# Moving every SBUF tile of a tuned encoder block to a multiple of 128 bytes

## Chip, cores and metric

The kernel runs on one core of a Trainium2 chip. The metric is the device time of one execution in microseconds (us), as the median of several runs.

## What is computed

One block of a streaming encoder on 1024 tokens of 1024 channels, with 16 meta tokens in front, in float32. Cut to what matters:

```python
def hybrid_mixer(u, w_in, ...):
    a, q, k, v, r, lr, ga, gb = jnp.split(einsum('bld,dn->bln', u, w_in), IN_SPLITS, axis=-1)
    p = multiscale_pool(a)                       # trailing means over 2, 4, 8, 16 positions, minus the token
    y_a = (p @ w_pool_mix, per group, * pool_scale) @ w_pool_out
    log_a = log_sigmoid(lr @ w_gate_up + b_gate) / GLA_TAU
    o = gla_chunked(q * GLA_DK ** -0.5, k, v, log_a)      # 4 heads, chunks of 64
    y_b = (rmsnorm(o, gla_norm) * silu(r)) @ w_gla_out
    return (sigmoid(ga) * y_a + sigmoid(gb) * y_b) @ w_out

def reference(x, meta_tokens, ...):
    h = concatenate([meta, x])
    h = h + hybrid_mixer(rmsnorm(h, norm_mix), ...)
    h = h + square(relu(rmsnorm(h, norm_ffn) @ w_ff1)) @ w_ff2        # 1024 -> 4096 -> 1024
    return rmsnorm(h, norm_final)[:, N_META:]
```

## The kernel before

Every large product is made of float32r matmuls. A float32 operand is split into a rounded part and the rest (`hi`, `lo`; ScalarE copies, VectorE or GpSimd subtracts), and `mm3` (L248) issues three matmuls for one product: L252 hi times hi, L253 hi times lo, L254 lo times hi. The first operand is the weights that are loaded into the array, 128x128; the second moves through it, mostly 128x512. Each matmul loads its weights anew. An output tile is one PSUM bank, 128x512 (`b_sc`, `b_mm`, `b_y`, `b_z`, `b_o`). In the profile a row reads output<-inputs, with the moving operand first or the two sorted together, and a tile that is both is named once.

The stages follow one another in the list `one`, and TensorE's order is written out by hand (`tc.manual_schedule` for PE):

1. `start`, `gate_stage` (to about 220 us): the norm, transposes of x into `th`, `tl`, and the blocks ga, q, r and two of gb, as a Strassen-like scheme of seven products for each pair of blocks (`Quarters`): moving operands are `th0`/`tl0` behind their 16 meta columns, `th1`/`tl1`, and the combinations `P4` to `P7`; weights are the splits in `w1h`, `w1l`.
2. The pooling branch (to about 310 us): `a_block` with 264- and 512-wide pieces of `th`, `mix_block`, `ya_block` with `pm` as the moving operand.
3. `gla` (to about 500 us): the chunked attention, with the blocks k, v, gb and `yb_block` (moving operand `yg`) poured between its steps.
4. `out_tile` (to about 640 us): `wo0`, then `wo1` move, `th`, `tl` are the weights.
5. `ff_layers` (to about 935 us): the first layer of the MLP in `Quarters` again; moving are `th0`, `th1`, `wo0` (reused) and `t4h`, `t4l`; weights `w1h`, `w1l`.
6. `ff2` (to the end): seven products of the second layer; both operands are splits in a ring of seven slots, four in `w1h`, `w1l` and three in `fxh`, `fxl`, so that either may be moving or weights.

SBUF is laid out by two stacks (`Stack`, L35): `left` grows up from the start, `right` down from the end; a tile's address is what was pushed before it. The sizes in a partition that matter here:

```python
ident = left.push("ident", [P, P], F32)          # 512 bytes in a partition
mask = left.push("mask", [P, 6, CH], U8)         # 384
gB = left.push("gB", [P, D], F32)                # 4096
small = left.push("small", [P, 152], F32)        # 608
wgu = left.push("wgu", [16, 256], F32)           # 1024
metab = left.push("metab", [P, 4, 16], F32)      # 256
lrT_meta = left.push("lrT_meta", [16, 16], F32)  # 64
```

Behind them on the left come `raw0`, `raw1`, `w1h`, `w1l`, `th0`, `tl0`, `th1`, `tl1`, and then each stage's tiles; in the first two stages `lrtok` (576 bytes) lies ahead of the others. In the built program `ident` begins at byte 16512, `w1h` at 31648, `th0` at 48032, `P5h` at 123872; the right stack ends at byte 229344, with `fxh` at 219104 and `t4h` at 202720.

Of the kernel before, what the change touches and what calls it, by code (L numbers as in the profile page):

```python
# [7 lines left out]
F32 = mybir.dt.float32  # L8
# [6 lines left out]
P = 128  # L15
# [88 lines left out]
def kernel(  # L104
# [10 lines left out]
    act, dve, pool, pe = nc.scalar, nc.vector, nc.gpsimd, nc.tensor  # L115
    left, right = Stack(tc, "left"), Stack(tc, "right")

    psp, ps_open = {}, []

    def banks(keep=0, **tags):  # L120
# [35 lines left out]
    ident = left.push("ident", [P, P], F32)  # L156
    mask = left.push("mask", [P, 6, CH], U8)
    gB = left.push("gB", [P, D], F32)
    small = left.push("small", [P, 152], F32)
    small_at = [0]  # L160

    def tiny(n):
        a = small_at[0]
        small_at[0] += n
        assert small_at[0] <= 152
        return small[:, a : a + n]

    pscale, bgate, gnorm = tiny(4), tiny(2), tiny(4)
    stat = [tiny(16) for _ in range(4)]
    eps_t = tiny(1)  # L170
    pool.memset(eps_t, EPS)
    wgu = left.push("wgu", [16, 256], F32)
    metab = left.push("metab", [P, 4, 16], F32)
    lrT_meta = left.push("lrT_meta", [16, 16], F32)
    raw = Raw(nc, [left.push(f"raw{i}", [P, D], F32) for i in range(2)])
    W1 = Ring(nc, raw, left.push("w1h", [P, 2, D], F32R), left.push("w1l", [P, 2, D], F32R), 2)
    left_ff = left.mark()
# [14 lines left out]
    def bcast(v):  # L192
        return v[None, :].broadcast_to([P, D])
# [27 lines left out]
    def layer_norm(xt, u):  # L221

        rows = xt.shape[0]
        ss = ln_stat[ln_n[0] % 4][:rows]
        ln_n[0] += 1
        act.activation(u, xt, ACT.Square, accum_out=ss)
        rs = inv_sqrt(ss, 1, 1.0 / D)
        dve.scalar_tensor_tensor(u, xt, rs, gB[:rows], ALU.mult, ALU.mult)
# [3 lines left out]
    def transposed(u, half, at, tags=("ms",), to=None):  # L232
        rows = u.shape[0]
        th, tl = (t[half] for t in to or (TH, TL))
        if rows == P:
            for j in range(2):
                turn_n[0] += 1
                b = bank(tags[turn_n[0] % len(tags)]).rearrange("p (a b) -> p a b", a=4)
                for i in range(4):
                    pe.transpose(b[:, i], u[:, (4 * j + i) * P : (4 * j + i + 1) * P], ident)  # L240
                split_from_psum(th[:, 4 * j : 4 * j + 4, at : at + P], tl[:, 4 * j : 4 * j + 4, at : at + P], b)
        else:
            b = bank("ms")[:, : 8 * rows].rearrange("p (a b) -> p a b", a=8)
            for i in range(8):
                pe.transpose(b[:, i], u[:, i * P : (i + 1) * P], ident[:rows, :rows])
            split_from_psum(th[:, :, at : at + rows], tl[:, :, at : at + rows], b)
# [38 lines left out]
    class Quarters:  # L285
# [9 lines left out]
        def load(self, i, u):  # L295
            dst = self.places[i % 2][u]
            self.w[i, u] = dst.rearrange("p (k c) -> p k c", k=KT)
            nc.sync.dma_start(self.w[i, u], self.block(2 * i + u))
# [103 lines left out]
    S, rings = {}, [W1]  # L402
# [9 lines left out]
    def drive(steps):  # L412

        for ring, aps, fn in steps:
            if fn not in (start, gate_stage):
                for r in rings:
                    r.top_up()
            wbs = [ring.views.pop(ring.done + i) for i in range(len(aps))] if ring else []
            held = len(aps)
            for cost in fn(*wbs) or ():  # L420
                if cost == "free":
                    ring.done, held = ring.done + held, 0
                    for r in rings:
                        r.top_up()
                else:
                    yield cost
            if ring:
                ring.done += held
# [16 lines left out]
    def load_vw(i):  # L445
        vw, n = S["vw"][i], 256 + 16 * (i == 0)
        for j in range(2):
            r = raw.load(w_cols(C_V + i * 256 + j * P), D).rearrange("p (k c) -> p k c", k=KT)
            c = slice(j * P, (j + 1) * P)
            act.activation(vw[:, 0, :, c], r, ACT.Copy)  # L450
            eng = pool if i else dve
            eng.tensor_tensor(vw[:, 1, :, c], r, f32(vw[:, 0, :, c]), ALU.subtract)
        if i == 0:
            r = S["lrraw"]
            act.activation(vw[:, 0, :, 256:], r, ACT.Copy)
            pool.tensor_tensor(vw[:, 1, :, 256:], r, f32(vw[:, 0, :, 256:]), ALU.subtract)
# [3 lines left out]
    def v_tile(i, t):  # L460

        vw, w = S["vw"][i], 256 + 16 * (i == 0)
        if t == 8:
            half, at, n = 0, 0, META
        else:
            half, n = t // 4, P
            at = OFF[half] + (t % 4) * P
        b = bank("mm")[:n, :w]
        mm3(
            b, KT, lambda k: (TH[half][:, k, at : at + n], TL[half][:, k, at : at + n]),  # L470
            lambda k: (vw[:, 0, k], vw[:, 1, k]),
        )
        if i == 0:
            dve.tensor_copy(S["lrtok"][:n, t], b[:, 256:])
        if t == 8:
            act.activation(vm[:, i * 256 : i * 256 + 256], b[:, :256], ACT.Copy)
        else:
            act.activation(S["v"][i][:, t], b[:, :256], ACT.Copy)
# [27 lines left out]
    def turned(u, t):  # L506

        half, at = t // 4, OFF[t // 4] + (t % 4) * P
        for j in range(2):
            b = quad(bank("ms"))  # L510
            for i in range(4):
                pe.transpose(b[:, i], u[:, (4 * j + i) * P : (4 * j + i + 1) * P], ident)
            k = slice(4 * j, 4 * j + 4)
            split_from_psum(TH[half][:, k, at : at + P], TL[half][:, k, at : at + P], b)
            act.activation(S["ut"][half, j][:, :, (t % 4) * P : (t % 4 + 1) * P], b, ACT.Copy)

    def start():
        act.preload_act_table_set("natural_log_exp_and_others")
        S["lrtok"] = left.push("lrtok", [P, 9, 16], F32)
        S["lrraw"] = left.push("lrraw", [P, KT, 16], F32)  # L520
        S["left_x"] = left.mark()
        xs = left.push("xs", [P, 4, D], F32)
        us = left.push("us", [P, 3, D], F32)
        xm = left.push("xm", [META, D], F32)
        um = left.push("um", [META, D], F32)
        mf = left.push("mf", [P, 6, CH], F32)
        S["u2p"] = right.push("u2p", [P, 2, HALF], F32)
        S["fs"] = right.push("fs", [P, 2, HALF], F32)
        q = gate_quarters
        for i in range(2):  # L530
            q.places[i][0] = right.push(f"rawx{i}", [P, D], F32)
        S["right_ut"] = [right.mark()]
        S["ut"] = {}
        for half, j in ((0, 1), (1, 0), (1, 1), (0, 0)):
            S["ut"][half, j] = right.push(f"ut{half}{j}", [P, 4, HALF], F32)
            S["right_ut"].append(right.mark())
        S["vw"] = [right.push("vw0", [P, 2, KT, VP], F32R)]
        load = lambda t: nc.sync.dma_start(xs[:, t % 4], x[t * P : (t + 1) * P, :])
        load(0)
        nc.sync.dma_start(ident, ident_in)  # L540
        nc.sync.dma_start(gB, bcast(norm_mix))
        for t in (1, 2, 3):
            load(t)
        q.load(0, 0)
        m = lambda half, j: tuple(a[half][:, 4 * j : 4 * j + 4, OFF[half] : OFF[half] + HALF] for a in (TH, TL))
        q.x.update({"P1": m(0, 0), "P2": m(0, 1), "P3": m(1, 1)})
        run = S["gate_run"] = q.run()
        for t in range(8):
            if t < 4:
                layer_norm(xs[:, t % 4], us[:, t % 3])  # L550
                turned(us[:, t % 3], t)
                load(t + 4)
                if t == 0:
                    nc.sync.dma_start(S["lrraw"], w_in[:, C_LR : C_LR + 16].rearrange("(k p) c -> p k c", p=P))
                    load_vw(0)
                    q.load(1, 0)
                continue
            if t == 4:
                nc.sync.dma_start(xm, meta)
                q.load(0, 1)  # L560
                q.load(1, 1)
                nc.sync.dma_start(mf, masks)
                q.prime()
                next(run)
                next(run)
                v_tile(0, 0)
            layer_norm(xs[:, t % 4], us[:, t % 3])
            turned(us[:, t % 3], t)
            if t < 7:
                v_tile(0, t - 3)  # L570
            else:
                layer_norm(xm, um)
        next(run)
        transposed(um, 0, 0)
        next(run)
        v_tile(0, 8)
        pool.tensor_copy(mask, mf)
# [78 lines left out]

    one = []
    step(one, start)
    step(one, gate_stage)

# [841 lines left out]
```

## Time and profile before

| | |
|---|---|
| median of 3 runs | 1262.49 us (1261.29 to 1262.67) |
| profiled execution | 1260.3 us, of which the span from first to last instruction 1258.5 us |
| granted TensorE clock, mean | 0.997 |
| TensorE matmuls | 6799, busy 97% of the span |
| VectorE, ScalarE, GpSimd busy | 68%, 50%, 5% |
| DMA | 175.40 MB, 139 GB/s over the span |

The profile is that of one execution. A matmul's busy time is from its start to its modelled end, and matmuls overlap, so the rate of TensorE is read from the distance between starts. A row of groups gives the line, engine, operation, output<-inputs, shapes and count, then the busy time in us and the mean of one in ns, then the idle time ahead of it and what ended that.

### The profile page before, as it was taken

To read this page: it belongs to the slowest core of one execution; us is meant where nothing else is said; L and a number is where in the kernel's file an instruction comes from. 1 tells how busy PE (TensorE), PEld (TensorE's weight loads), DVE (VectorE), ACT (ScalarE), POOL (GpSimd) and SP (SyncE) were. 2 spreads that over 40 slices of the span, in tenths; PEclk is the share of its full clock that TensorE was granted. 3 is DMA by queue.
4 is the path that set the end of the run, shared out by engine and by line. 5 is a ranking of instruction groups with operands and counts; after the bars stand their busy time and mean duration, and the time that the engine had idled before them with its cause. 6 is when DMAs were issued, how large, how long until landed. Compare 5 with 4: busy or idle time off the path is not lost.

```text
span 1258.5 us, 18159 instructions
## 1 busy us (share of the span) xinstructions
PE 1216.6 (97%) x6799; PEld 1001.1 (80%) x6799; DVE 852.4 (68%) x1404; ACT 625.3 (50%) x1101; POOL 58.6 (5%) x37
## 2 busy tenths in 40 slices
PE   3999999999999999999999999999999999999997
PEld 2888888988887787788878888888878788888776
DVE  6776667564365767743897676677764887887686
ACT  7567757431445564422664554554553444445444
POOL 0000000001000115400000000000000000000000
PEclk9999999999999999999999999999999999999999
DMA  8023334427211236851244444543569863323432
GB/s 264 1 67 109 109 95 136 130 70 241 75 35 35 85 116 203 310 175 51 76 143 149 161 151 142 163 155 130 175 228 373 277 213 102 100 93 92 167 92 84
DMA packets 143863, 175.40 MB, mean 139 GB/s; under 512 B 11008, under 2 KB 83472, under 8 KB 143776
## 3 DMA queue, kind: packets, MB, share of 16 engines
q1 hardware_dynamic: 143776, 174.25, 42.7%
q8 instruction: 53, 0.87, 0.3%
q14 instruction: 34, 0.28, 0.1%
HBM read 120.74 MB, written 53.48 MB: 138 GB/s over the span
## 4 chain that ended last, share of the span: by engine, by line
PE 90%; DVE 4%; ACT 2%; DMA 2%; issue 2%; SPq 0%; DVEq 0%; ACTq 0%
PE b_mm L252 9%; PE b_mm L254 9%; PE b_mm L253 9%; PE b_o L253 8%; PE b_o L254 8%; PE b_o L252 8%; PE b_y L252 5%; PE b_y L254 5%; PE b_y L253 5%; PE b_z L252 3%; PE b_z L253 3%; PE b_z L254 3%; PE b_sc L252 3%; PE b_sc L253 3%; PE b_sc L254 3%
## 5 line engine op out<-in xcount | busy, mean ns | idle before, releaser
L252 PE MATMUL b_mm<-th,w1h 128*128 128x512 f32 (+1 forms) x240 | 86.0, 358 | 0.0
L253 PE MATMUL b_mm<-tl,w1h 128*128 128x512 f32 (+1 forms) x240 | 83.8, 349 | 0.0
L254 PE MATMUL b_mm<-th,w1l 128*128 128x512 f32 (+1 forms) x240 | 83.7, 349 | 0.0
L270 ACT ACTIVATE w1h<-raw 128x512 fp32r<-128x512 f32 x96 | 59.6, 623 | 44.0 <-PE b_sc L253 14.2
L252 PE MATMUL b_sc<-th,w1h 128*128 128x512 f32 x192 | 76.7, 399 | 1.9 <-ACT u2p L362 1.9
L252 PE MATMUL b_o<-w1h 128*128 128x512 f32 x192 | 75.3, 392 | 2.7 <-DVE h L1310 1.7
L253 PE MATMUL b_o<-w1l,w1h 128*128 128x512 f32 x192 | 75.0, 390 | 1.3 <-DVE w1l L271 1.3
L253 PE MATMUL b_sc<-tl,w1h 128*128 128x512 f32 x192 | 75.8, 395 | 0.3 <-DVE tl L197 0.3
L254 PE MATMUL b_sc<-th,w1l 128*128 128x512 f32 x192 | 75.7, 394 | 0.0
L254 PE MATMUL b_o<-w1h,w1l 128*128 128x512 f32 x192 | 75.1, 391 | 0.1
L271 DVE TENSOR_TENSOR w1l<-raw,w1h 128x512 fp32r<-128x512 f32 x96 | 65.7, 686 | 11.1 <-ACT w1h L270 11.1
L270 ACT ACTIVATE w1h<-fs 128x512 fp32r<-128x512 f32 x72 | 45.4, 630 | 49.9 <-PE b_y L253 34.3
L252 PE MATMUL b_z<-th,w1h 128*128 128x512 f32 x160 | 62.5, 390 | 0.4 <-DVE c L616 0.4
L253 PE MATMUL b_z<-tl,w1h 128*128 128x512 f32 x160 | 62.4, 390 | 0.4 <-DVE tl L1222 0.4
L254 PE MATMUL b_z<-th,w1l 128*128 128x512 f32 x160 | 62.3, 389 | 0.0
L271 DVE TENSOR_TENSOR w1l<-fs,w1h 128x512 fp32r<-128x512 f32 x72 | 49.4, 686 | 16.2 <-ACT w1h L270 16.1
L1373 DVE TENSOR_TENSOR bt<-w,w 128x512 f32<-128x512 f32 x80 | 54.8, 686 | 2.2 <-DMA w<-in_w_ff_dram 2.2
L270 ACT ACTIVATE w1h<-bt 128x512 fp32r<-128x512 f32 x44 | 27.6, 629 | 55.3 <-issue 31.9
L252 PEld LDWEIGHTS b_mm<-th,w1h 128*128 128x128 f32 x240 | 45.0, 188 | 8.8 <-issue 2.3
L252 PE MATMUL b_mm<-wo,th 128*128 128x512 f32 x128 | 50.7, 396 | 0.0
L254 PE MATMUL b_o<-fxh,fxl 128*128 128x512 f32 x128 | 50.2, 392 | 0.0
L252 PE MATMUL b_o<-fxh 128*128 128x512 f32 x128 | 50.1, 392 | 0.0
(334 smaller groups left out, 3388.7 us busy)
## 6 DMA issues: line engine op xcount, KB each, us to landing
hf_dram<-h SPq DMA_DIRECT2D x112, 256.0 KB, 2.1
raw<-hf_dram SPq DMA_DIRECT2D x112, 256.0 KB, 2.7
w<-in_w_ff_dram SPq DMA_DIRECT2D x64, 256.0 KB, 4.8
raw<-in_w_in_dram SPq DMA_DIRECT2D x24, 512.0 KB, 4.7
raw<-in_w_ff_dram SPq DMA_DIRECT2D x16, 512.0 KB, 4.2
rawx<-in_w_ff_dram SPq DMA_DIRECT2D x16, 512.0 KB, 4.2
xs<-in_x_dram SPq DMA_DIRECT2D x8, 512.0 KB, 6.1
rawx<-in_w_in_dram SPq DMA_DIRECT2D x8, 512.0 KB, 4.5
```

Source lines behind the costliest of these rows:

```text
L252: pe.matmul(ps, ah, bh, start=first and i == 0, stop=False, skip_group_check=more)
L253: pe.matmul(ps, ah, bl, start=False, stop=False, skip_group_check=more)
L254: pe.matmul(ps, al, bh, start=False, stop=last and i == n - 1, skip_group_check=more)
L270: act.activation(hi, a, ACT.Copy)
L271: dve.tensor_tensor(lo, a, f32(hi), ALU.subtract)
L1373: dve.tensor_tensor(bt, w, S["w2"][q[3:]][:, i], ALU.add if q[2] == "+" else ALU.subtract)
```

## The change

Three tiles change in size and one is added. `small` shrinks from 152 to 128 floats (of which the kernel uses fewer), `lrT_meta` gets 32 columns of which 16 are used, `lrtok` gets a tenth row that is not used, and a tile of 24 floats (96 bytes) is put at the end of SBUF ahead of the right stack and never touched. So all tiles begin at multiples of 128 bytes: `w1h` at 31616, `th0` at 48000, `P5h` at 123904, `fxh` at 219008, `t4h` at 202624. The pieces of `th0` behind the meta columns still begin 64 bytes into a row, and its rows are 2112 bytes apart.

```diff
@@ -115,6 +115,8 @@
     left, right = Stack(tc, "left"), Stack(tc, "right")
 
+    ctx.enter_context(tc.tile_pool(name="p_edge", bufs=1, side="right")).tile([P, 24], F32, name="edge")
+
     psp, ps_open = {}, []
@@ -156,13 +158,13 @@
-    small = left.push("small", [P, 152], F32)
+    small = left.push("small", [P, 128], F32)
     small_at = [0]
 
     def tiny(n):
         a = small_at[0]
         small_at[0] += n
-        assert small_at[0] <= 152
+        assert small_at[0] <= 128
         return small[:, a : a + n]
@@ -171,7 +173,7 @@
     metab = left.push("metab", [P, 4, 16], F32)
-    lrT_meta = left.push("lrT_meta", [16, 16], F32)
+    lrT_meta = left.push("lrT_meta", [16, 32], F32)[:, :16]
@@ -516,7 +518,7 @@
         act.preload_act_table_set("natural_log_exp_and_others")
-        S["lrtok"] = left.push("lrtok", [P, 9, 16], F32)
+        S["lrtok"] = left.push("lrtok", [P, 10, 16], F32)
         S["lrraw"] = left.push("lrraw", [P, KT, 16], F32)
```

## The prediction, made before the changed kernel ran

> **What bounds it.** I read the page's busy shares first, then its chain, then the groups of TensorE by shape, then start times in the timeline.
>
> ```profile
> PE 1216.6 (97%) x6799; PEld 1001.1 (80%) x6799; DVE 852.4 (68%) x1404; ACT 625.3 (50%) x1101; POOL 58.6 (5%) x37
> ...
> PE 90%; DVE 4%; ACT 2%; DMA 2%; issue 2%; SPq 0%; DVEq 0%; ACTq 0%
> ```
>
> TensorE is busy 97% of the span, and 90% of the chain that ended last is TensorE work. DMA and waits for other engines make up the rest, so what moves the time is how fast one matmul follows the next. "Busy" does not show that, since matmuls overlap; the distance from one start to the next does. Here are four starts from the last stage (`ff2`), columns start, duration (us), engine, line, output<-inputs:
>
> ```profile
> 1194.63 0.39 PE L252 MATMUL b_o<-w1h 128*128 128x512 f32 x1
> ...
> 1196.67 0.39 PE L252 MATMUL b_o<-fxh 128*128 128x512 f32 x1
> ...
> 1199.43 0.39 PE L252 MATMUL b_o<-w1h,fxh 128*128 128x512 f32 x1
> ...
> 1202.23 0.40 PE L252 MATMUL b_o<-w1h 128*128 128x512 f32 x1
> ```
>
> From 1194.63 to 1196.67 stand 9 matmuls with both operands in w1h and w1l: 2.04 us, 226.7 ns each. From 1199.43 to 1202.23 stand 12 with one operand in w1 and the other in fxh or fxl: 2.80 us, 233.3 ns each. The shape is the same, the stage is the same, and no wait is shown.
>
> What differs is the place in the partition. From the pushes in the code: up to `small` every left tile has a multiple of 128 bytes; `small` has 608 (96 over), `lrT_meta` 64, so raw0, w1h, w1l, th, tl, wo0 and all left tiles behind them begin 32 bytes past a multiple of 128. `lrtok` (576) moves what follows it in the first two stages to 96 past. Tiles of the right stack end at the end of SBUF, which is 96 past, so fx, t4, pm, yg and wo1 begin at 96. Same remainder: 226.7 ns. Remainders 64 apart: up to 233.3.
>
> The groups by shape say the same over all 1258 us; their mean duration goes with the distance (389 where the distance is 226.7, 395 where it is 233):
>
> ```profile
> L252 PE MATMUL b_y<-wo,w1h 128*128 128x512 f32 x128 | 49.8, 389 | 0.0
> L253 PE MATMUL b_y<-wo,w1h 128*128 128x512 f32 x128 | 49.8, 389 | 0.0
> L254 PE MATMUL b_y<-wo,w1l 128*128 128x512 f32 x128 | 49.8, 389 | 0.0
> L252 PE MATMUL b_o<-w1h,fxh 128*128 128x512 f32 x64 | 25.2, 394 | 0.0
> L253 PE MATMUL b_o<-w1l,fxh 128*128 128x512 f32 x64 | 25.2, 394 | 0.0
> L254 PE MATMUL b_o<-w1h,fxl 128*128 128x512 f32 x64 | 25.3, 395 | 0.0
> L252 PE MATMUL b_o<-fxh,w1h 128*128 128x512 f32 x64 | 25.3, 395 | 0.0
> L253 PE MATMUL b_o<-fxl,w1h 128*128 128x512 f32 x64 | 25.1, 392 | 0.5 <-DVE small L213 0.5
> L254 PE MATMUL b_o<-fxh,w1l 128*128 128x512 f32 x64 | 25.2, 394 | 0.0
> L252 PE MATMUL b_y<-t4h,w1h 128*128 128x512 f32 x64 | 25.3, 395 | 0.0
> L253 PE MATMUL b_y<-t4l,w1h 128*128 128x512 f32 x64 | 25.0, 390 | 0.0
> L254 PE MATMUL b_y<-t4h,w1l 128*128 128x512 f32 x64 | 25.1, 393 | 0.0
> ```
>
> wo0 with w1 (both at 32) has 389 in all three lines; the pairs across the stacks have 390 to 395.
>
> **The change, part by part.** It adds and removes no instruction. In the built program every engine has the same instructions in the same order with the same waits; only addresses move: left tiles by 32 bytes, right tiles by 96. No queue is passed and no wait is added. So each term is a change of duration.
>
> *Pairs across the stacks* get equal remainders (w1h at 31616, fxh at 219008, t4h at 202624: all multiples of 128) and should take the 389 of the wo0 rows. w1 against fx weights: 64 x (5+5+6) = 1.0 us. fx against w1 weights: 64 x (6+3+5) = 0.9 us. t4: 64 x (6+1+4) = 0.7 us. The other three pairs across the stacks, pm and yg against w1 weights and wo1 against th weights, have 3 x 64 matmuls each; I take t4's 0.7 us for each, since their own rows hold waits too: 2.1 us. Together 4.7 us.
>
> *Finding the rhythm again.* Rows with equal remainders that follow such pairs lie above 389:
>
> ```profile
> L252 PE MATMUL b_o<-w1h 128*128 128x512 f32 x192 | 75.3, 392 | 2.7 <-DVE h L1310 1.7 <-ACT w1h L270 1.0
> L253 PE MATMUL b_o<-w1l,w1h 128*128 128x512 f32 x192 | 75.0, 390 | 1.3 <-DVE w1l L271 1.3
> L254 PE MATMUL b_o<-w1h,w1l 128*128 128x512 f32 x192 | 75.1, 391 | 0.1
> ```
>
> w1 against w1: 192 x (3+1+2) = 1.2 us, with both operands at 32, as wo0 and w1 have. Such a row comes after the pairs w1 against fx each round, so a slow rhythm seems to outlast the pair that brought it. The idle columns show that part of it follows waits, which stay; I take 1.0 us.
>
> *The first-half blocks and P4 to P7 in `gate_stage`* stay as they are. P4 to P7 lie at 96 behind `lrtok` and go to 0 (P5h from 123872 to 123904), but w1h goes to 31616, so they are now 128 apart modulo 256, where they were 64 apart. The slices of th0 behind the 16 meta columns keep every distance to w1 that they had (64 bytes on, 2112 from row to row).
>
> ```profile
> 197.31 0.40 PE L252 MATMUL b_y<-P7h,w1h 128*128 128x512 f32 x1
> ...
> 205.71 0.40 PE L252 MATMUL b_sc<-th,w1h 128*128 128x512 f32 x1
> 206.41 0.40 PE L252 MATMUL b_sc<-th,w1h 128*128 128x512 f32 x1
> 207.11 0.39 PE L252 MATMUL b_sc<-th,w1h 128*128 128x512 f32 x1
> ```
>
> P7, P5 and P4: 36 matmuls in 8.40 us, 233.3 ns each, at a distance of 64. At 206.41 begin three with th0's second row, 128 from w1 modulo 256: 0.70 us to 207.11, again 233.3. So 384 matmuls of P4 to P7 keep their price; bounds are 384 x 6.6 ns = 2.5 us less (the 226.7 of equal remainders), and, to the other side, as much more. I take zero, as the nearest row does.
>
> *DMA and the vector engines.* No row separates a load's rate from its destination's place; DMA holds 2% of the chain, 25 us, of which a change of 2% would be 0.5 us either way: zero. For VectorE the same line on raw (32) and on rawx (96) shows what remainders cost:
>
> ```profile
> L271 DVE TENSOR_TENSOR w1l<-raw,w1h 128x512 fp32r<-128x512 f32 x96 | 65.7, 686 | 11.1 <-ACT w1h L270 11.1
> L271 DVE TENSOR_TENSOR w1l<-rawx,w1h 128x512 fp32r<-128x512 f32 x40 | 27.7, 694 | 19.9 <-ACT w1h L270 19.9
> ```
>
> 1% on an engine that is idle a third of the time, hidden behind the matmuls of the stage: zero. If that cover were gone, 40 x 8 ns = 0.3 us.
>
> *Sum.* 4.7 + 1.0 = 5.7 us of TensorE time; by the chain's 90%, 5.1 us. The profiled execution took 1260.3 us (span 1258.5 and 1.8 around it), 2.2 under the median of 1262.49; 1260.3 becomes 1255.2, and the median 1257.4. By its own terms this case reaches from 1254 (P4 to P7 gain too, nothing is lost beside the chain) to 1260.5 (P4 to P7 lose, and a stage gives its gain back in waits for w1h).
>
> **Rivals.**
>
> *Only the difference of places counted so far; the place itself counts too, and 0 is better than 32.* All 512-wide products of lines 252 to 254 have both operands 32 or 96 past a multiple of 128, so before does not show them at 0. There are 4,584 (all such rows of the groups, the largest x192, the smallest x4):
>
> ```profile
> L252 PE MATMUL b_sc<-th,w1h 128*128 128x512 f32 x192 | 76.7, 399 | 1.9 <-ACT u2p L362 1.9
> ...
> L253 PE MATMUL b_sc<-ph,mw 128*128 128x512 f32 x4 | 1.6, 388 | 0.0
> ```
>
> One more step of the size seen (233.3 to 226.7) would be 4,584 x 6.6 ns = 30 us: 1227 with the gain above; a quarter step 1250. For it: the step exists. Against it: 32 and 96 give the same 226.7 to 227 (w1 against w1, fx against fx). The nearest row with a moving operand at 0 is the 264-wide product of th0:
>
> ```profile
> 259.00 0.28 PE L252 MATMUL b_mm<-th,w1h 128*128 128x264 f32 x1
> ...
> 261.90 0.29 PE L252 MATMUL b_mm<-th,w1h 128*128 128x264 f32 x1
> ...
> 264.85 0.39 PE L252 MATMUL b_mm<-th,w1h 128*128 128x512 f32 x1
> ```
>
> 24 matmuls with slices at 32 and 96 in turn take 2.90 us, 24 with slices at 64 and 0 take 2.95. A moving operand at 0 gains nothing beside weights at 32. Chance 0.16. [...]
>
> *Worse at 0.* The same unseen place, the other sign: with both operands at 0 the weight load and the moving operand could lock into the slow rhythm that 233.3 shows, in `ff1`, `ff2` and everywhere else. Full step: 1262.5 - 5.1 + 30 = 1287; a quarter step, which is the size I would expect, 1262.5 - 5.1 + 7.5 = 1265. It decides from 5.1 us / 4,584 = 1.1 ns per matmul upwards. For it: the 0 and 64 slices are 2 ns slower per matmul than the 32 and 96 ones. Against it: there it is the mixture with weights at 32 that costs. Chance 0.17.
>
> *No effect at all.* The difference between rows would come from what was running at the time, not from addresses: 1262.5. For it: remainders of pairs and stages are partly the same thing. Against it: 226.7 and 233.3 within 8 us of one stage. Chance 0.15. [...]
>
> **Numbers.** Forecast 0.52: 1257.4, its own range 1254 to 1260.5. A measurement here can tell about 0.2%, 2.5 us, from no change. Faster by more: 0.52 less 0.03 for its upper end, and the better place 0.16: 0.65. Within: that 0.03, and most of no effect: 0.16. Slower: 0.17 and 0.02 of no effect: 0.19. The range goes down to 1240, half of the better place, and up to 1270, most of the worse one.
>
> **What would show it.** Right: in the groups, w1 against fx, t4, pm, yg and wo1 at 389 to 390, and b_o with equal remainders at 389 to 390; b_y<-wo,w1h still at 389; P7, P5, P4 still 233.3 apart. Wrong: b_y<-wo,w1h away from 389 (the place itself counts), or pairs across the stacks still at 393 to 395 (addresses are not the cause), or idle times of TensorE before L252 grown by what the pairs gained.

## The result and the profile after

| | median | runs | profiled execution | span |
|---|---|---|---|---|
| before | 1262.28 us | 6, 1261.29 to 1263.46 | 1260.3 us | 1258.5 us |
| changed | 1256.34 us | 6, 1255.74 to 1256.53 | 1256.4 us | 1254.6 us |

The ratio is 0.9952 (95% interval 0.9941 to 0.9964): 5.9 us, or 0.5%, faster. The forecast was 1257.4 us. The mean granted TensorE clock was 0.998, against 0.997 before.

The page of the changed kernel, busy shares and the shares of the chain of waits:

```profile
PE 1212.4 (97%) x6799; PEld 1001.8 (80%) x6799; DVE 850.0 (68%) x1404; ACT 625.4 (50%) x1101; POOL 57.5 (5%) x37
...
PE 90%; DVE 4%; ACT 2%; DMA 2%; issue 2%; SPq 0%; DVEq 0%; ACTq 0%
```

The picture is the same as before: same counts, same shares, TensorE still 90% of the chain. TensorE's busy sum is 4.2 us lower, the span 3.9 us. The groups by shape say where (the lines of the changed file are 2 higher: 252 to 254 are now 254 to 256):

```profile
L254 PE MATMUL b_y<-wo,w1h 128*128 128x512 f32 x128 | 49.8, 389 | 0.0
L254 PE MATMUL b_o<-w1h,fxh 128*128 128x512 f32 x64 | 24.9, 389 | 0.0
L255 PE MATMUL b_o<-w1l,fxh 128*128 128x512 f32 x64 | 24.9, 389 | 0.0
L256 PE MATMUL b_o<-w1h,fxl 128*128 128x512 f32 x64 | 24.9, 389 | 0.0
L254 PE MATMUL b_o<-fxh,w1h 128*128 128x512 f32 x64 | 24.9, 389 | 0.0
L255 PE MATMUL b_o<-fxl,w1h 128*128 128x512 f32 x64 | 25.0, 391 | 0.7 <-DVE small L215 0.7
L256 PE MATMUL b_o<-fxh,w1l 128*128 128x512 f32 x64 | 24.9, 389 | 0.0
L254 PE MATMUL b_y<-t4h,w1h 128*128 128x512 f32 x64 | 24.9, 389 | 0.0
L255 PE MATMUL b_y<-t4l,w1h 128*128 128x512 f32 x64 | 24.9, 389 | 0.0
L256 PE MATMUL b_y<-t4h,w1l 128*128 128x512 f32 x64 | 24.9, 389 | 0.0
L254 PE MATMUL b_o<-w1h 128*128 128x512 f32 x192 | 75.0, 390 | 2.8 <-DVE h L1312 1.8 <-ACT w1h L272 1.0
L255 PE MATMUL b_o<-w1l,w1h 128*128 128x512 f32 x192 | 75.0, 390 | 1.4 <-DVE w1l L273 1.4
L256 PE MATMUL b_o<-w1h,w1l 128*128 128x512 f32 x192 | 74.8, 390 | 0.1
L254 PE MATMUL b_mm<-yg,w1h 128*128 128x512 f32 x64 | 26.3, 411 | 1.4 <-ACT w1h L75 1.4
L254 PE MATMUL b_y<-P7h,w1h 128*128 128x512 f32 x32 | 12.6, 394 | 0.0
L254 PE MATMUL b_sc<-th,w1h 128*128 128x512 f32 x192 | 76.8, 400 | 2.0 <-ACT u2p L364 2.0
```

The pairs across the stacks have gone from 390 to 395 down to the 389 that wo with w1 had all along and still has. The row that stays at 391 is the one with a wait ahead of it (0.7 us on `small`). P7 stays at 394, where it had 396. In the timeline of `ff2`, the same stretch as in the prediction:

```profile
1193.40 0.39 PE L254 MATMUL b_o<-fxh 128*128 128x512 f32 x1
...
1196.12 0.39 PE L254 MATMUL b_o<-w1h,fxh 128*128 128x512 f32 x1
...
1198.84 0.39 PE L254 MATMUL b_o<-w1h 128*128 128x512 f32 x1
...
1201.56 0.39 PE L254 MATMUL b_o<-fxh,w1h 128*128 128x512 f32 x1
```

12 matmuls lie between each two of these starts: fx with fx, w1 with fx, w1 with w1. Each stretch takes 2.72 us, 226.7 ns a matmul; before, the first one took 2.76 and the middle one 2.80. Nothing tells the pair across the stacks from its neighbours any more.

### The profile page after: what moved, and what is told of

The parts are those of the page before. It is cut to its first block, busy times and chain, and to the rows that moved or that the text cites. A ratio compares the mean times of both kernels' runs of the same rounds, so it can differ in the third digit from the quotient of the medians.

```text
span 1254.6 us, 18159 instructions
## 1 busy us (share of the span) xinstructions
PE 1212.4 (97%) x6799; PEld 1001.8 (80%) x6799; DVE 850.0 (68%) x1404; ACT 625.4 (50%) x1101; POOL 57.5 (5%) x37
## 4 chain that ended last, share of the span: by engine, by line
PE 90%; DVE 4%; ACT 2%; DMA 2%; issue 2%; SPq 0%; DVEq 0%; ACTq 0%
PE b_mm L254 9%; PE b_mm L256 9%; PE b_mm L255 9%; PE b_o L255 8%; PE b_o L256 8%; PE b_o L254 8%; PE b_y L254 5%; PE b_y L255 5%; PE b_y L256 5%; PE b_z L254 3%; PE b_z L255 3%; PE b_z L256 3%; PE b_sc L255 3%; PE b_sc L254 3%; PE b_sc L256 3%
## 5 line engine op out<-in xcount | busy, mean ns | idle before, releaser
L256 PE MATMUL b_o<-w1h,w1l 128*128 128x512 f32 x192 | 74.8, 390 | 0.1
L256 PEld LDWEIGHTS b_mm<-th,w1l 128*128 128x128 f32 x240 | 45.1, 188 | 6.0
```

The costliest lines, as they stand in the source:

```text
L256: pe.matmul(ps, al, bh, start=False, stop=last and i == n - 1, skip_group_check=more)
```

## The experiments

The theory: what counts is the distance between the addresses of a matmul's two operands (start of the moving operand minus start of the weights, within a partition), and equal remainders give the quick rhythm. Rivals: the multiple of 128 itself counts (alignment); or something in the stages, and no address. In each variant of the kernel TensorE and the other engines have the same instructions in the same order as the changed kernel; only addresses differ.

### Equal remainders without the multiple of 128

`e1_strip64`: the kernel before with nothing but a strip at the end of SBUF. The right tiles move to 32 past a multiple of 128, where the left ones already are.

```diff
+    ctx.enter_context(tc.tile_pool(name="p_edge", bufs=1, side="right")).tile([P, 16], F32, name="edge")
```

> The kernel before with one edit: a strip of 64 bytes at the end of SBUF, so that the right stack's tiles begin 32 bytes past a multiple of 128, as the left ones do; nothing lies at a multiple of 128 that did not before, and lrtok stays as it was. Theory A (only the distance of the two operands counts): the pairs across the stacks (w1 against fx, t4, pm, yg, wo1) go to 389 ns busy and the time to 1256.5 (1255.5 to 1258). Theory B (lying at a multiple of 128 is what helps): the pairs stay at 392 to 395 and the time at 1262.3. P4 to P7 keep 394 to 396 under both.

Measured: 1257.15 us (1255.38 to 1258.1), ratio 0.9959 (0.9947 to 0.9972). Groups by shape:

```profile
L254 PE MATMUL b_o<-w1h,fxh 128*128 128x512 f32 x64 | 24.9, 389 | 0.0
L256 PE MATMUL b_y<-t4h,w1l 128*128 128x512 f32 x64 | 24.9, 389 | 0.0
L254 PE MATMUL b_y<-P7h,w1h 128*128 128x512 f32 x32 | 12.7, 396 | 0.0
```

The whole gain, with neither w1, th and wo nor fx and t4 at a multiple of 128. One strip of 64 bytes does what the four edits do; the P's keep the 396 of before, as their distance to w1 does.

### Multiples of 128, but 128 apart

`e2_far128`: the changed kernel with `lrT_meta` taken from `small`, so that all left tiles behind it lie 128 bytes earlier. Everything is at a multiple of 128, but left and right are 128 apart modulo 256.

```diff
-    lrT_meta = left.push("lrT_meta", [16, 32], F32)[:, :16]
+    lrT_meta = tiny(16)[:16]
```

> The changed kernel with lrT_meta put into small, so that the left tiles begin 128 bytes earlier: every tile still lies at a multiple of 128, but left and right tiles are 128 apart modulo 256, where they were 0 apart. Theory A in the form that the distance counts modulo 256: the pairs across the stacks go back to 392 to 396 and the time to 1261 to 1264. Theory A modulo 128, or theory B: 389 and 1256.3.

Measured: 1262.56 us (1260.35 to 1263.8), ratio 1.0002 (0.9993 to 1.0011).

```profile
L254 PE MATMUL b_o<-w1h,fxh 128*128 128x512 f32 x64 | 25.2, 394 | 0.0
L256 PE MATMUL b_y<-t4h,w1l 128*128 128x512 f32 x64 | 25.3, 395 | 0.0
L254 PE MATMUL b_o<-w1h 128*128 128x512 f32 x192 | 75.2, 392 | 2.8 <-DVE h L1312 1.8 <-ACT w1h L272 1.0
```

All the gain is gone, although every tile is aligned. So alignment to 128 bytes is worth nothing by itself, and equal remainders modulo 128 are not enough; that the period is 256 the map below shows. The third row, w1 with w1, did not change its own distance; it is back at 392, as the step of the rhythm had it.

### The same distances, elsewhere

`e3_all32`: the tiles behind `lrT_meta` and those of the right stack 32 past a multiple of 128, with the distances of the changed kernel.

```diff
-    ctx.enter_context(tc.tile_pool(name="p_edge", bufs=1, side="right")).tile([P, 24], F32, name="edge")
+    ctx.enter_context(tc.tile_pool(name="p_edge", bufs=1, side="right")).tile([P, 16], F32, name="edge")
-    lrT_meta = left.push("lrT_meta", [16, 32], F32)[:, :16]
+    lrT_meta = left.push("lrT_meta", [16, 40], F32)[:, :16]
```

> The changed kernel with lrT_meta 32 bytes longer and the strip 32 bytes shorter, so that every distance between tiles is as in the changed kernel, but all lie 32 bytes past a multiple of 128. Theory A: 1256.3 (within 1), pairs at 389. Theory B: 1262, pairs at 392 to 395.

Measured: 1256.6 us (1255.58 to 1258.07), ratio 0.9957 (0.9943 to 0.997), the pairs at 389:

```profile
L254 PE MATMUL b_o<-fxh,w1h 128*128 128x512 f32 x64 | 24.9, 389 | 0.0
```

Whether the tiles lie at 32 or at 0 does not count.

### Only half of the change

`e6_left_only`: the changed kernel without the strip. Left tiles at multiples of 128, right tiles 96 past.

```diff
-    ctx.enter_context(tc.tile_pool(name="p_edge", bufs=1, side="right")).tile([P, 24], F32, name="edge")
```

> The changed kernel without the strip: left tiles at multiples of 128, right tiles 96 past one. Theory A, by the map: right tiles moving against left weights stand at 96 (233.3 ns), w1 moving against fx weights at 160 (234.3 ns): 960 x 6.6 + 192 x 7.6 = 7.8 us over the changed kernel and 1 to 2 us for finding the rhythm, 1264 to 1266, slower than before, whose distance was 64 (228.9). Theory B: half of the tiles lie at multiples of 128, so between 1256 and 1262.

Measured: 1264.71 us (1263.74 to 1266.63), ratio 1.0025 (1.0015 to 1.0035): slower than before. Here the matmul lines are 252 to 254:

```profile
L252 PE MATMUL b_o<-w1h,fxh 128*128 128x512 f32 x64 | 25.3, 395 | 0.0
L254 PE MATMUL b_y<-t4h,w1l 128*128 128x512 f32 x64 | 25.5, 398 | 0.0
```

Aligning half of the tiles is worse than aligning none. It moves the distance from 64 to 96 where a right tile moves (fx, t4), and from 192 to 160 where w1 moves against fx. The t4 row goes from 393 to 398; from start to start t4's matmuls have a mean of 234.6 ns, where they had 230.3.

### The disputed cost by itself

`e4_map`: none of the block is computed. ScalarE makes a tile of weights `w` and a tile `m`; TensorE runs groups of 24 matmuls, 512 columns each; each group starts at another pair of offsets, and one ScalarE copy follows it, beside the first matmuls of the next group. Nothing else runs beside the matmuls.

```diff
+WOFF = (0, 8, 16, 24)
+MOFF = tuple(range(0, 128, 8))
...
+        for wo in WOFF:
+            for mo in MOFF:
+                run(512, wo, mo, at)
```

Offsets are in floats of 4 bytes, `wo` of the weights and `mo` of the moving operand; `run` issues one group.

> None of the block is computed: 24 float32r matmuls of 128x512 for each of 4 starts of the weights (0, 32, 64, 96 bytes) by 16 starts of the moving operand (0 to 480 bytes in steps of 32), rows of 4096 bytes and weights 512 bytes apart, with no VectorE and no DMA beside them; then four groups of 128x256. Theory A: the distance between starts depends on moving minus weights, 226.7 ns where it is 0 modulo 128 or 256, up to 233.3 elsewhere, the same for all four starts of the weights. Theory B: the groups with both at 0 are the quickest, those with weights at 32 or 96 slower whatever the moving operand. No effect of addresses: all alike.

The ScalarE timeline around the first groups (columns start, duration, engine, line, operation; in brackets the idle time before it and its releaser):

```profile
42.08 0.60 ACT L67 ACTIVATE res<-b 128x512 f32<-128x512 f32 x1 [4.84 <-PE b L66]
47.52 0.60 ACT L67 ACTIVATE res<-b 128x512 f32<-128x512 f32 x1 [4.84 <-PE b L66]
53.12 0.60 ACT L67 ACTIVATE res<-b 128x512 f32<-128x512 f32 x1 [5.00 <-PE b L66]
58.63 0.60 ACT L67 ACTIVATE res<-b 128x512 f32<-128x512 f32 x1 [4.91 <-PE b L66]
64.24 0.60 ACT L67 ACTIVATE res<-b 128x512 f32<-128x512 f32 x1 [5.01 <-PE b L66]
```

Between two copies lies one group: distance 0 took 5.44 us (226.7 ns a matmul), 32 took 5.60 (233.3), 64 took 5.51 (229.6), 96 took 5.61 (233.8). The first matmuls of a group still settle; over the last 15 starts the distance, moving operand minus weights modulo 256, gives

| distance, bytes | 0 | 32 | 64 | 96 | 128 | 160 | 192 | 224 |
|---|---|---|---|---|---|---|---|---|
| ns from start to start | 226.7 | 233.3 | 228.9 | 233.3 | 233.6 | 234.3 | 233.3 | 233.3 |

The four places of the weights (0, 32, 64, 96) give the same figures to within 0.3 ns, and so do a distance and the same plus 256. So 256 is the period, 0 the best of these values, and 64 the next. With nothing but ScalarE's copies running beside, "something in the stages" is out as well.

`e7_map_fine`: the same with weights at 0 and steps down to 4 bytes, and with fewer columns.

> None of the block is computed: weights at 0, moving operand 4 to 252 bytes further on in steps finer than 32 at 512 columns, then 384, 272, 264 and 256 columns at 0 to 224 bytes in steps of 32. [...] Open: whether some finer distance is quicker, and whether 0 is the quickest at fewer columns too.

Copies behind the groups at the distances 0, 4 and 8, then 24 and 28 bytes (a group lies between its own row and the row ahead of it):

```profile
36.17 0.60 ACT L66 ACTIVATE res<-b 128x512 f32<-128x512 f32 x1 [4.84 <-PE b L65]
41.85 0.60 ACT L66 ACTIVATE res<-b 128x512 f32<-128x512 f32 x1 [5.08 <-PE b L65]
47.44 0.60 ACT L66 ACTIVATE res<-b 128x512 f32<-128x512 f32 x1 [4.99 <-PE b L65]
...
69.86 0.60 ACT L66 ACTIVATE res<-b 128x512 f32<-128x512 f32 x1 [5.00 <-PE b L65]
75.30 0.60 ACT L66 ACTIVATE res<-b 128x512 f32<-128x512 f32 x1 [4.84 <-PE b L65]
```

Distance 4 takes 5.68 us (236.7 ns each), 8 takes 5.59, 28 takes 5.44, as quick as 0. Over the last 15 starts 28, 60 and 252 have 226.7, while 4, 20, 24 and 240 have 236.6, 240.0, 233.3 and 236.9. So steps of 4 bytes matter (20, 24 and 28: 240.0, 233.3, 226.7), in no simple order. Nothing was quicker than 226.7. At 384 columns 0, 32 and 64 all have 173.3, the others up to 176.8. At 256 columns 0 is not the best:

```profile
211.93 0.39 ACT L66 ACTIVATE res<-b 128x264 f32<-128x264 f32 x1 [2.49 <-PE b L65]
214.81 0.39 ACT L66 ACTIVATE res<-b 128x256 f32<-128x256 f32 x1 [2.48 <-PE b L65]
...
229.01 0.39 ACT L66 ACTIVATE res<-b 128x256 f32<-128x256 f32 x1 [2.43 <-PE b L65]
231.73 0.38 ACT L66 ACTIVATE res<-b 128x256 f32<-128x256 f32 x1 [2.34 <-PE b L65]
```

24 matmuls of 256 columns at distance 0 take 2.88 us (120.0 ns each), at 192 only 2.72 (113.3).

### What is left of the mechanism

`e8_map_cols`: the map with weights of 128, 96, 64 and 32 columns, to see whether the amount of weights loaded makes the rhythm.

```python
pe.matmul(b[:c], W[:, w : w + c], M[:, r % 8, mo : mo + 512], ...)   # shortened; c is 128, 96, 64, 32 in turn
```

> None of the block is computed: the map again at 512 columns and 8 distances (0 to 224 bytes), with weights of 128, 96, 64 and 32 columns. [...]

At distance 0: 226.6, 229.9, 229.3 and 231.9 ns. The spread over the eight distances shrinks with the columns (7.7, 5.4, 4.2, 3.0 ns), the level does not. So the spread goes with the amount of weights; what the level goes with is not shown. With fewer weight columns 0 is no longer the best distance either: 192 has 228.1 ns at 96 columns, 64 has 228.5 at 64, and 224 has 230.3 at 32.

`e11_map_next`: the starts alternate from one matmul to the next, by k = 32, 64, 96 or 128, so that a matmul's distance to its own weights and that to the next one's differ.

```diff
+                for ws, ms in (((0, k), (0, k)), ((0, k), (k, 0)), ((0, k), (0, 0)), ((0, 0), (0, k))):
+                    run(ws, ms, at)
```

`ws` and `ms` are the two starts of the weights and of the moving operand, in floats, taken in turn.

> None of the block is computed: 512 columns, 128 weight columns, and starts that alternate from one matmul to the next by k = 32, 64, 96 or 128 bytes. First, weights and moving operand of one matmul shift together (distance to its own weights 0, to the next matmul's k or -k); second, they shift against each other (distance to its own k or -k, to the next one's weights 0); third, only the weights alternate; fourth, only the moving operand. If it is the load of the next weights that meets the moving operand, the second kind has 226.7 ns and the first 229 to 234; if the matmul's own weights count, the other way round.

```profile
30.60 0.60 ACT L66 ACTIVATE res<-b 128x512 f32<-128x512 f32 x1 [4.84 <-PE b L65]
36.04 0.60 ACT L66 ACTIVATE res<-b 128x512 f32<-128x512 f32 x1 [4.84 <-PE b L65]
41.62 0.60 ACT L66 ACTIVATE res<-b 128x512 f32<-128x512 f32 x1 [4.98 <-PE b L65]
47.16 0.60 ACT L66 ACTIVATE res<-b 128x512 f32<-128x512 f32 x1 [4.94 <-PE b L65]
```

Constant starts: 5.44 us. Alternating by 32 with the own distance 0: 5.58; with the next one's distance 0: 5.54. Over the last 15 starts the own distance 0 gave 231.7, 231.7, 234.2 and 228.4 ns for the four k, the next one's 230.0, 231.9, 230.4 and 230.0. Neither keeps 226.7, and no other alternation tried does (228.4 to 234.7 ns). Whether the distance to a matmul's own weights or that to the next one's makes the cost is not settled by these runs.

### The version that the map points to

`e5_p_near`: the changed kernel with two more rows in `lrtok`, which put P4 to P7 at distance 0 from w1 instead of 128.

```diff
-        S["lrtok"] = left.push("lrtok", [P, 10, 16], F32)
+        S["lrtok"] = left.push("lrtok", [P, 12, 16], F32)
```

> The changed kernel with two more rows in lrtok (768 bytes instead of 640), so that P4 to P7 begin 128 bytes later and lie at a distance of 0 from w1h modulo 256, where they were 128 from it. Theory A (distance modulo 256, by the map): P4 to P7 go from 394 to 397 ns busy to 389 to 390, 384 x (233.6 - 226.7) = 2.6 us at most, 2 us as the rows of the changed kernel stand (232 ns): 1254.3, within 1253.5 to 1255. Theory B (multiples of 128): nothing changes, 1256.3.

Measured: 1253.87 us (1252.95 to 1257.81), ratio 0.9938 (0.9925 to 0.9951).

```profile
L254 PE MATMUL b_y<-P7h,w1h 128*128 128x512 f32 x32 | 12.5, 390 | 0.0
L256 PE MATMUL b_y<-P7h,w1l 128*128 128x512 f32 x32 | 12.4, 389 | 0.0
```

The twelve rows of P4 to P7 sum to 149.4 us, against 151.6 in the changed kernel and 151.9 before. The 2.5 us against before are the bound that the prediction gave to these matmuls. To compare it with the changed kernel both ran once more, side by side:

> The changed kernel itself, beside the next one on the same chip: 1256.3, 0.5% under the kernel before.

> The changed kernel with lrtok of 768 bytes (P4 to P7 at a distance of 0 from w1h modulo 256), again: 1254.2, 2 us under the changed kernel, by the 384 matmuls at 389 to 390 ns instead of 394 to 397.

`e9_after_again`: 1256.22 us (1254.35 to 1257.22); `e10_p_near_again`: 1255.26 us (1252.04 to 1255.38), with the same 149.4 us in the P rows. Ratios to before 0.9957 (0.9943 to 0.9971) and 0.9946 (0.9933 to 0.9959). The median was lower both times, by 2.5 us (against the changed kernel in another set of runs) and by 1.0 us, and the rows show why; the intervals of the ratios overlap, so the difference of the times is not clear of noise, while that of the rows, 2.2 us, came both times. It has the lowest median of the versions measured.

## Why the prediction was right

**What bounds it.** TensorE's start-to-start distance, not waits: right. Busy sum and span fell together (4.2 and 3.9 us), and the idle columns did not grow by what the pairs gained.

**Pairs across the stacks.** Sums of the rows, all three lines of each pair, in us:

| rows | before | changed | difference | predicted |
|---|---|---|---|---|
| w1h,fxh and its two others | 75.7 | 74.7 | 1.0 | 1.0 |
| fxh,w1h and its two others | 75.6 | 74.8 | 0.8 | 0.9 |
| t4 with w1 | 75.4 | 74.7 | 0.7 | 0.7 |
| pm with w1 | 75.5 | 75.1 | 0.4 | 0.7 |
| wo (b_mm) with th | 150.5 | 150.1 | 0.4 | 0.7 |
| yg with w1 | 77.8 | 77.8 | 0.0 | 0.7 |
| w1 with w1, `b_o` | 225.4 | 224.8 | 0.6 | 1.0 |
| fx with fx, `b_o` | 150.2 | 149.5 | 0.7 | not in the sum |
| P4 to P7 | 151.9 | 151.6 | 0.3 | 0 |
| th0 in `b_sc` (`gate_stage` and `ff_layers`) | 228.2 | 228.9 | -0.7 | 0 |

The three pairs whose rows were read carry what was read from them. The term that was mis-sized is the borrowed one: 0.7 us for each of pm, yg and wo1, 2.1 together, where 0.8 came. Their own means before (pm's sum of 75.5 is 393 over 192 matmuls) would have allowed no more than 0.8 for pm; and yg's rows, at 411 ns in the costliest, waited for the ring of weights in both kernels: 1.3 us for w1h and 1.1 for w1l before, 1.4 and 1.1 in the changed kernel, with the sum at 77.8 in both. Where nothing waits, the three came down as well: from start to start (260 ns or more left out) pm went from 229.1 to 227.2 ns, wo with th from 228.2 to 227.1, yg from 229.6 to 228.4. So the sign that the prediction named, 389 to 390 in all these rows, held for the pairs that it had read (one row at 391, behind a wait) and not for these three. One more pair across the stacks, vw with th at 256 and 272 columns, has no term in the prediction; its rows of 64 went from 110.1 us to 110.3, so nothing was missed by that.

**Finding the rhythm again.** 1.0 us was taken, for w1 with w1, and 0.6 came there. Another 0.7 came in fx with fx, which the prediction's sum leaves out; that both together, 1.3, lie near 1.0 is luck. `e2_far128` shows the effect by itself: w1 with w1 goes back to 392 when only its neighbours are moved. Nor does it need a pair at another distance ahead of it. At 1236.79 us of the trace of before, `ff2` steps from w1 with w1 to fx with fx, equal remainders both, and the starts are 229, 229, 233, 236, 224, 231, 236, 228, 233, 231 ns apart before they settle at 226 to 227. So it is the step between tiles 64 apart that costs. `e4_map` has a shorter way from a distance of 224 to one of 0: 235, 230, 236, 228, 232, 231 ns, then 227.

**P4 to P7, zero.** Right here, but the reason held only in part. The prediction read P7, P5 and P4 in one stretch, 233.3 ns each, as the price of the distance 64. In the same trace the last P7 and P4 of the stage, at the same distance, are quicker:

```profile
213.99 0.39 PE L252 MATMUL b_y<-P7h,w1h 128*128 128x512 f32 x1
...
219.48 0.40 PE L252 MATMUL b_z<-th,w1h 128*128 128x512 f32 x1
```

24 matmuls take 5.49 us, 228.8 ns each, and their starts are 229, 232 and 226 ns apart in turn, as in the map at 64. P6, t4 and fx moving against w1, all at 64, settle to the same three. The P7 behind slices of th0, and the P5 and P4 behind it, run 233, 233 and 234 ns apart instead, as the map does at 192. So one distance can hold two rhythms, 228.8 and 233.3 ns, with different matmuls ahead of them; what decides between the two is open. (The pair that the prediction read at 233.3 in `ff2`, w1 moving against fx, stands at 192 and not at 64: the sign of the distance counts, with 233.3 ns at 192 and 228.9 at 64 in `e4_map`.) Over the whole trace the P's had means of 230.4 to 232.3 ns before and 231.6 to 232.9 in the changed kernel, so 64 and 128 cost about the same by the mixture of rhythms, not because 64 has one price. That there is a gain at distance 0, and its size of 2.2 to 2.5 us, `e5_p_near` shows.

**The th0 slices, zero.** `b_sc` lost 0.7 us that was not foreseen, but not by the distance of its operands. In `ff_layers` its rows gained 0.6. In the first 60 us they lost 1.3: at the very start of `gate_stage` matmuls follow one another at 425 to 428 ns, four before and nine in the changed kernel, so the first twelve took 5.72 us (from 28.26 to 33.98) before and 6.67 (from 27.92 to 34.59) in the changed kernel. `e1_strip64`, where w1 has the distances to th0 and the P's that it has before, has these nine too. The granted clock reads 1.00 in that window in both; what ends the slow stretch is not shown.

**DMA and the vector engines, zero.** VectorE's busy sum went from 852.4 to 850.0 us, and DMA's share of the chain stayed at 2%.

**Sum.** 5.7 us were summed, 5.1 after the chain's share. The table's differences add up to 4.2, as TensorE's busy sum on the page does; by the chain's 90% that is 3.8, and the span fell by 3.9. That this agrees is no proof of the 90%. By place: where the same matmul of line 254 starts in both traces, the changed kernel was 0.8 us late at 220 us, 0.6 late at 633, 0.7 early at 938 and 3.8 early at 1245. So most of the loss is that of the first twelve matmuls of `b_sc`, and what was gained behind it came through in the main: the last step, 3.1 us in `ff2`, is the 1.0 and 0.8 of w1 with fx and the 1.3 of the rhythm. The term that was too large is the borrowed 2.1, of which 0.8 came.

The median gave 5.9 us (4.5 to 7.4 by the interval of the ratio), 2 us more than the traces. The profiled execution of before took 1260.3 us, 2 below its median; that of the changed kernel, 1256.4, lay at its median. Single runs of before in later comparisons went from 1259.74 to 1263.66, so 2 us is within what one execution differs from another; what differs in it stays open. That the median came within 1.1 us of the forecast is therefore partly luck: the terms that the traces show add up to less than was forecast, and the medians moved by more.

**The rivals.** *The place itself counts*, better or worse at 0: `b_y<-wo,w1h`, whose operands both moved from 32 to 0, has 389 before and after, and `e3_all32` puts everything back to 32 with no loss (1256.6). Both are out. *No effect of addresses*: out by `e2_far128`, where 128 bytes undo the whole gain (1262.56), and by `e4_map`: with nothing but ScalarE's copies beside, moving one operand's start alone makes 226.7 ns into up to 234.3.

## What to carry to other kernels

For back-to-back fp32r matmuls of 512 columns these runs say: place the moving operand and the weights so that their addresses in the partition are equal modulo 256 (226.7 ns, against 228.9 to 234.3 at the other multiples of 32 in `e4_map`), and so too all tiles that take these parts one after another (1.3 us of the traced gain stand in rows whose own distance did not change). Alignment to 128 bytes does not do it (1262.56) and is not needed (1257.15), and aligning one side alone can cost (1264.71). Read the mean of each operand pair in the groups by shape: a pair that lies some ns over another of the same shape, with no wait ahead, is to be checked in the timeline from start to start. For other column counts measure first, since 256 columns had their best distance at 192 (113.3 ns, against 120.0 at 0, in `e7_map_fine`).

## What the runs showed of the hardware

- The distance between a matmul's two operands (float32r, moving minus weights) changed its rate by up to 3% at 512 columns by steps of 32 bytes (`e4_map`: 226.7 to 234.3 ns), by up to 6% at steps of 4 bytes (`e7_map_fine`: 240.0 at 20 bytes). In `e4_map` a distance and the same plus 256 bytes gave the same figures to within 0.3 ns.
- The best distance of those tried depended on the number of columns (`e7_map_fine`): 0 for 512 (28, 60 and 252 equal it, 226.7 ns), 0, 32 and 64 alike for 384 (173.3 ns), 192 for 256 (113.3 against 120.0 ns at 0).
- One distance can hold two rhythms: at 64 the kernel before has 228.8 ns a matmul in one stretch (213.99 to 219.48 us) and 233.3 in another (197.31 to 205.71 us), with different matmuls ahead of them.
- After a step to tiles at another remainder the starts were uneven for six matmuls in `e4_map` (228 to 236 ns, then 227) and for ten in `ff2` before (224 to 236 ns, then 226 to 227), so such a step costs quick pairs too (0.7 and 0.6 us of the gain here stand in rows whose own distance did not change).
- 226.7 ns at 512 columns did not fall with fewer columns of weights (`e8_map_cols`, at distance 0: 226.6 ns at 128 columns, 229.9 at 96, 229.3 at 64, 231.9 at 32), and with 128 columns of weights no distance tried in `e4_map` and `e7_map_fine` came below it. What sets this figure is open.
